# Row sums of a 64 MB tensor: 16-row loads from two queues, and a finely cut last buffer

## Chip, cores, metric

One core of a Trainium2 chip is used. The metric is the device time of one execution, in microseconds (us), as the median of several runs.

## The reference

```python
def setup_inputs():
    batch, seq, dim = 32, 512, 1024
    return {"x": np.random.randn(batch, seq, dim).astype(np.float32)}

def reference(x):
    return np.sum(x, axis=-1).astype(np.float32)
```

There are 16,384 rows of 1,024 floats, 67.1 MB. Each of the 128 partitions gets 128 consecutive rows. The result is 64 KB.

## The kernel before

Fifteen tiles of 8 rows a partition (4 MB each) are loaded by one queue, that of SyncE, into four buffers. VectorE sums four rows of each tile in one reduction, ScalarE the other four, one activation with an accumulator a row. The sixteenth tile is loaded row by row, and the two engines take the rows in turn.

```python
    G = 8
    ...
    T = C // G              # C = 128 rows a partition, so 16 tiles
    DVE_N = 4
    ...
    xpool = ctx.enter_context(tc.tile_pool(name="x", bufs=4))
    ...                     # res, and the two helpers: one activation a row; one reduction of n rows
    for t in range(T):
        xt = xpool.tile([P, G, D], x.dtype, tag="xt")
        c0 = t * G
        if t < T - 1:
            nc.sync.dma_start(out=xt, in_=x_t[t])
            reduce_cols_dve(xt[:, 0:DVE_N], c0, DVE_N)
            for j in range(DVE_N, G):
                reduce_col_act(xt[:, j], c0 + j)
        else:
            for j in range(G):
                nc.sync.dma_start(out=xt[:, j], in_=x_t[t, :, j])
            ...             # even rows on ScalarE, odd rows on VectorE
    nc.sync.dma_start(out=out2d, in_=res)
```

A scheduler puts the instructions of each engine into an order of its own, within what the data dependences allow.

Of the kernel before, what the change touches and what calls it, by code (L numbers as in the profile page):

```python
# [1 line left out]

# [4 lines left out]


@with_exitstack
def kernel(  # L10
    ctx: ExitStack,
    tc: tile.TileContext,
    x: bass.AP,
    out: bass.AP,
):
    nc = tc.nc
    P = nc.NUM_PARTITIONS

    x_flat = x.flatten_outer_dims()
    R, D = x_flat.shape  # L20
    assert R % P == 0
    C = R // P

    G = 8
    assert C % G == 0
    T = C // G
    DVE_N = 4

    x_t = x_flat.rearrange("(p t j) d -> t p j d", p=P, j=G)

    out2d = out.rearrange("a (b c) -> (a b) c", c=C)

    xpool = ctx.enter_context(tc.tile_pool(name="x", bufs=4))
    rpool = ctx.enter_context(tc.tile_pool(name="res", bufs=1))

    res = rpool.tile([P, C], mybir.dt.float32)

    def reduce_col_act(xt_col, c):
        nc.scalar.activation(  # L39
            out=xt_col,  # L40
            in_=xt_col,
            func=mybir.ActivationFunctionType.Copy,
            accum_out=res[:, c : c + 1],
        )

    def reduce_cols_dve(xt_cols, c0, n):
        nc.vector.tensor_reduce(  # L47
            out=res[:, c0 : c0 + n],
            in_=xt_cols,
            axis=mybir.AxisListType.X,  # L50
            op=mybir.AluOpType.add,
        )

    for t in range(T):
        xt = xpool.tile([P, G, D], x.dtype, tag="xt")
        c0 = t * G
        if t < T - 1:
            nc.sync.dma_start(out=xt, in_=x_t[t])  # L58
            reduce_cols_dve(xt[:, 0:DVE_N], c0, DVE_N)
            for j in range(DVE_N, G):  # L60
                reduce_col_act(xt[:, j], c0 + j)
        else:
            for j in range(G):
                nc.sync.dma_start(out=xt[:, j], in_=x_t[t, :, j])
            for j in range(G):
                if j % 2 == 0:
                    reduce_col_act(xt[:, j], c0 + j)
                else:
                    reduce_cols_dve(xt[:, j], c0 + j, 1)

    nc.sync.dma_start(out=out2d, in_=res)


# [1 line left out]
_INS = ['x']  # L75
_OUTS = [((32, 512), 'float32')]


# [23 lines left out]
```

## Time and profile before

| what | value |
|---|---|
| time, median | 165.22 us (165.18 to 165.25) |
| profiled span | 163.7 us |
| VectorE busy, ScalarE busy | 71.0 us, 69.6 us (43% each) |
| interval between landings of 4 MB tiles | 9.73 us, so 431 GB/s |

The first fence is the part of the page that cuts the span into 40 equal slices. A digit is the busy share of a slice in tenths; DMA is the mean share of the 16 DMA engines, and GB/s is what they moved.

```profile
DVE  0006337091551907337090642808245190733952
ACT  3006337091551907336091642808145190733960
DMA  6999999999999999999999999999999999998980
GB/s 200 432 432 440 416 448 416 416 432 424 424 424 440 416 448 424 416 456 424 432 442 416 448 416 424 448 432 432 432 424 448 416 424 448 424 432 364 407 349 16
```

The DMA row reads 8 or 9 from the second slice to the last but one; the two compute rows are full only in single slices, with nearly empty ones between. The second fence is the chain of work that ended last, by line, as shares of the span.

```profile
DMA xt<-in_x_dram 88%; DVE res L47 9%; SPq L58 1%
```

The waits view names the engine and tile that waited, what it waited for, the total in us, the count and the longest.

```profile
DVE res L47 <- DMA xt<-in_x_dram: 90.3, 17, 13.6
ACT xt L39 <- DMA xt<-in_x_dram: 89.6, 16, 11.5
```

Both compute engines spend some 90 us waiting for loads. The timeline gives start, duration, engine, line, operation, and in brackets the idle time before it and what ended it.

```profile
13.56 4.42 DVE L47 TENSOR_REDUCE res<-xt 128x4 f32<-128x4096 f32 x1 [13.56 <-DMA xt<-in_x_dram]
23.24 4.42 DVE L47 TENSOR_REDUCE res<-xt 128x4 f32<-128x4096 f32 x1 [5.26 <-DMA xt<-in_x_dram]
...
149.86 6.67 DVE L47 TENSOR_REDUCE res<-xt 128x4 f32<-128x4096 f32 x3 [5.30 <-DMA xt<-in_x_dram]
...
160.04 1.22 DVE L47 TENSOR_REDUCE res<-xt 128x1 f32<-128x1024 f32 x1 [1.28 <-DMA xt<-in_x_dram]
161.33 0.35 SPq L71 DMA_DIRECT2D out_dram<-res  x1
```

The tiles land 9.7 us apart and take 4.42 us to sum. After the last landing (160.04) there is one reduction of 1.22 us, and then the store. So the kernel is a load of 67 MB at 431 GB/s, with the DMA engines busy all the time (share 0.99 to 1.02 in the windows from 4 to 148 us), with a start of about 2 us and an end of about 4 us.

### The profile page before, as it was taken

The numbers are of one execution on the slowest core, as the hardware profiler recorded it, in microseconds if no ns is written. First come the engines' busy times: TensorE is split into PE (matmuls) and PEld (weight loads), VectorE is DVE, ScalarE is ACT, GpSimd is POOL, SyncE is SP. The second block draws the span as 40 slices with busy tenths as digits, with TensorE's granted clock in tenths as the row PEclk, the third lists the DMA queues.
The fourth block names the chain that finished last, engine by engine and source line by source line (L and its number), as shares of the span: only waits on it lengthen the run. The fifth ranks groups of instructions, "written<-read, shape, count | busy, mean of one in ns | idle before, by whom it ended". The sixth has DMA issues, their size and how long they took to land.

```text
span 163.7 us, 243 instructions
## 1 busy us (share of the span) xinstructions
DVE 71.0 (43%) x19; ACT 69.6 (43%) x129; POOL 0.2 (0%) x4
## 2 busy tenths in 40 slices
DVE  0006337091551907337090642808245190733952
ACT  3006337091551907336091642808145190733960
POOL 0000000000000000000000000000000000000000
DMA  6999999999999999999999999999999999998980
GB/s 200 432 432 440 416 448 416 416 432 424 424 424 440 416 448 424 416 456 424 432 442 416 448 416 424 448 432 432 432 424 448 416 424 448 424 432 364 407 349 16
DMA packets 3457, 67.18 MB, mean 410 GB/s; under 512 B 384, under 2 KB 512, under 8 KB 1536
## 3 DMA queue, kind: packets, MB, share of 16 engines
q1 hardware_dynamic: 3456, 67.18, 96.5%
q14 instruction: 1, 0.01, 0.0%
HBM read 67.11 MB, written 0.07 MB: 410 GB/s over the span
## 4 chain that ended last, share of the span: by engine, by line
DMA 88%; DVE 9%; SPq 1%; issue 0%
DMA xt<-in_x_dram 88%; DVE res L47 9%; SPq L58 1%
## 5 line engine op out<-in xcount | busy, mean ns | idle before, releaser
L47 DVE TENSOR_REDUCE res<-xt 128x4 f32<-128x4096 f32 (+1 forms) x19 | 71.0, 3745 | 90.3 <-DMA xt<-in_x_dram 90.3
L39 ACT ACTIVATE xt<-xt 128x1024 f32<-128x1024 f32 x64 | 66.8, 1044 | 89.6 <-DMA xt<-in_x_dram 89.6
L39 ACT ACTIVATION_READ_ACCUMULATOR xt<-xt 128x1 f32 x64 | 11.9, 187 | 0.0
L39 ACT ACT_TABLE_LOAD x1 | 1.3, 1283 | 0.7 <-PEq L86 0.7
L86 POOL MEMSET const-bfloat16-1.0<- 128x1 bf16 x1 | 0.1, 101 | 0.0
L86 POOL MEMSET const-uint8-127<- 128x1 uint8 x1 | 0.1, 101 | 0.0
L86 POOL MEMSET const-float32-0.0<- 128x1 f32 x1 | 0.1, 98 | 0.2 <-issue 0.2
L86 POOL MEMSET const-float32-1.0<- 128x1 f32 x1 | 0.1, 98 | 0.0
## 6 DMA issues: line engine op xcount, KB each, us to landing
xt<-in_x_dram SPq DMA_DIRECT2D x15, 4096.0 KB, 34.4
xt<-in_x_dram SPq DMA_DIRECT2D x8, 512.0 KB, 27.0
out_dram<-res SPq DMA_DIRECT2D x1, 64.0 KB, 1.5
```

What stands on the lines that cost most here:

```text
L39: nc.scalar.activation(out=xt_col, in_=xt_col, func=mybir.ActivationFunctionType.Copy, accum_out=res[:, c : c + 1],)
L47: nc.vector.tensor_reduce(out=res[:, c0 : c0 + n], in_=xt_cols, axis=mybir.AxisListType.X, op=mybir.AluOpType.add,)
L58: nc.sync.dma_start(out=xt, in_=x_t[t])
L86: nc = _bacc.Bacc("TRN2", target_bir_lowering=False, num_devices=1)
```

## The change

The intent was to use two issuing queues and larger transfers, and to make the work behind the last landing small. Tiles have 16 rows (8 MB) in three buffers, and the loads are issued in turn by SyncE and ScalarE. The last tile comes in pieces of 8, 4, 2, 1, 1/2, 1/4 and 1/4 rows. The last row is summed on VectorE by an operation that reads two streams, adds them and accumulates.

```diff
-    G = 8
+    G = 16
-    xpool = ctx.enter_context(tc.tile_pool(name="x", bufs=4))
+    xpool = ctx.enter_context(tc.tile_pool(name="x", bufs=3))
+    queues = [nc.sync, nc.scalar]
+    issued = []
+    def load(xt, c0, a, b):
+        q = queues[len(issued) % 2 if len(issued) < T else 0]
+        issued.append(a)
+        q.dma_start(out=xt[:, a:b], in_=x_p[:, c0 * D + a : c0 * D + b])
...
+    def pairs_dve(xt, a, b, first, acc):
+        h = (b - a) // 2
+        nc.vector.tensor_tensor_reduce(out=xt[:, a : a + h], in0=xt[:, a : a + h],
+            in1=xt[:, a + h : b], scale=1.0, scalar=first, op0=ADD, op1=ADD, accum_out=acc)
...
+    for t in range(T - 1):
+        ...
+        load(xt, c0, 0, G * D)
+        rows_dve(xt, c0, 0, G // 2)
+        rows_act(xt, c0, G // 2, G // 2)
...
+    for n in (8, 4, 2, 1):
+        load(xt, c0, j * D, (j + n) * D)
+        ...
+    cuts = [j * D + k for k in (0, D // 2, 3 * D // 4, D)]
+    for a, b in zip(cuts, cuts[1:]):
+        load(xt, c0, a, b)
...
+    for i, (a, b) in enumerate(zip(cuts, cuts[1:])):
+        pairs_dve(xt, a, b, acc[i - 1] if i else 0.0, acc[i])
```

Tiles 0, 2, 4 and 6 and the small pieces fall to SyncE. Tiles 1, 3 and 5 and the 8-row piece fall to ScalarE, which also sums rows. The scheduler's order on ScalarE, with L for a load and S for the eight row sums of a tile, is: L1, S0, S1, L3, S2, S3, S4, L5, L(8-row piece), S5, S6, and the sums of the pieces.

More of the change, by code (lines that the diff above doesn't have):

```diff
@@ L6 @@
 from concourse._compat import with_exitstack
+F32 = mybir.dt.float32
+ADD = mybir.AluOpType.add
 @with_exitstack
@@ L22 @@
     C = R // P
-    G = 8
+    x_p = x_flat.rearrange("(p c) d -> p (c d)", p=P)
+    out2d = out.rearrange("a (b c) -> (a b) c", c=C)
+    G = 16
     assert C % G == 0
     T = C // G
-    DVE_N = 4
-    x_t = x_flat.rearrange("(p t j) d -> t p j d", p=P, j=G)
-    out2d = out.rearrange("a (b c) -> (a b) c", c=C)
-    xpool = ctx.enter_context(tc.tile_pool(name="x", bufs=4))
+    xpool = ctx.enter_context(tc.tile_pool(name="x", bufs=3))
     rpool = ctx.enter_context(tc.tile_pool(name="res", bufs=1))
-    res = rpool.tile([P, C], mybir.dt.float32)
@@ L38, in reduce_col_act @@
-    def reduce_col_act(xt_col, c):
-        nc.scalar.activation(
-            out=xt_col,
-            in_=xt_col,
-            func=mybir.ActivationFunctionType.Copy,
-            accum_out=res[:, c : c + 1],
-        )
-    def reduce_cols_dve(xt_cols, c0, n):
-        nc.vector.tensor_reduce(
-            out=res[:, c0 : c0 + n],
-            in_=xt_cols,
-            axis=mybir.AxisListType.X,
-            op=mybir.AluOpType.add,
-        )
-    for t in range(T):
-        xt = xpool.tile([P, G, D], x.dtype, tag="xt")
+    res = rpool.tile([P, C], F32, name="res")
@@ new lines, with rows_dve @@
+    part = rpool.tile([P, 4], F32, name="part")
+    queues = [nc.sync, nc.scalar]
[4 more added lines that the diff above has]
+        q.dma_start(out=xt[:, a:b], in_=x_p[:, c0 * D + a : c0 * D + b])
+    def rows_dve(xt, c0, j, n):
+        nc.vector.tensor_reduce(
+            out=res[:, c0 + j : c0 + j + n],
+            in_=xt[:, j * D : (j + n) * D].rearrange("p (j d) -> p j d", d=D),
+            axis=mybir.AxisListType.X,
+            op=ADD,
+        )
@@ new lines, in rows_act @@
+    def rows_act(xt, c0, j, n):
+        for i in range(j, j + n):
+            v = xt[:, i * D : (i + 1) * D]
+            nc.scalar.activation(
+                out=v,
+                in_=v,
+                func=mybir.ActivationFunctionType.Copy,
+                accum_out=res[:, c0 + i : c0 + i + 1],
+            )
+    def pairs_dve(xt, a, b, first, acc):
+        h = (b - a) // 2
+        nc.vector.tensor_tensor_reduce(
+            out=xt[:, a : a + h],
+            in0=xt[:, a : a + h],
+            in1=xt[:, a + h : b],
+            scale=1.0,
+            scalar=first,
+            op0=ADD,
+            op1=ADD,
+            accum_out=acc,
+        )
@@ L56 @@
+    for t in range(T - 1):
         c0 = t * G
-        if t < T - 1:
-            nc.sync.dma_start(out=xt, in_=x_t[t])
-            reduce_cols_dve(xt[:, 0:DVE_N], c0, DVE_N)
-            for j in range(DVE_N, G):
-                reduce_col_act(xt[:, j], c0 + j)
-        else:
-            for j in range(G):
-                nc.sync.dma_start(out=xt[:, j], in_=x_t[t, :, j])
-            for j in range(G):
-                if j % 2 == 0:
-                    reduce_col_act(xt[:, j], c0 + j)
-                else:
-                    reduce_cols_dve(xt[:, j], c0 + j, 1)
+        xt = xpool.tile([P, G * D], F32, tag="xt", name="xt")
+        load(xt, c0, 0, G * D)
+        rows_dve(xt, c0, 0, G // 2)
+        rows_act(xt, c0, G // 2, G // 2)
@@ new lines @@
+    c0 = (T - 1) * G
+    xt = xpool.tile([P, G * D], F32, tag="xt", name="xt")
+    j = 0
+    runs = []
+    for n in (8, 4, 2, 1):
+        load(xt, c0, j * D, (j + n) * D)
+        runs.append((j, n))
+        j += n
+    cuts = [j * D + k for k in (0, D // 2, 3 * D // 4, D)]
+    for a, b in zip(cuts, cuts[1:]):
+        load(xt, c0, a, b)
+    for j, n in runs:
+        if n > 1:
+            rows_dve(xt, c0, j, n // 2)
+            rows_act(xt, c0, j + n // 2, n // 2)
+        else:
+            rows_act(xt, c0, j, 1)
@@ L71 @@
+    acc = [part[:, 0:1], part[:, 1:2], res[:, C - 1 : C]]
+    for i, (a, b) in enumerate(zip(cuts, cuts[1:])):
+        pairs_dve(xt, a, b, acc[i - 1] if i else 0.0, acc[i])
     nc.sync.dma_start(out=out2d, in_=res)
```

## The prediction

> **What bounds the kernel now.** Loads. In the chain of waits, 88% of the span (163.7 us) is the load of xt. VectorE and ScalarE are 43% busy each; the waits view puts their idle time (90.3 and 89.6 us) on that load. In the timeline a 4 MB load lands every 9.73 us (13.56 to 149.86, 14 intervals): 431 GB/s, with the DMA engines at about 1.00 share in the windows view. Only the ends are open: about 2 us before data flows, and after the last landing (160.02) one 1.22 us reduction and 2.4 us for the store. The eight pieces at the end run at about 408 GB/s.
>
> **What the change removes or adds.** At the ends, little: the last VectorE work shrinks from 1.22 to about 0.5 us (estimate); larger pieces save perhaps 0.3 us. About -1 us.
>
> What it moves is worse. An 8 MB load needs 19.5 us at 431 GB/s. [...] So two loads in flight land together, at half rate each, with one more in reserve (three buffers). Summing a tile takes about 8.7 us on VectorE (4.42 us per 4 rows) and 8.3 us on ScalarE (1.04 us a row).
>
> Moreover a load issued by ScalarE sits in its instruction stream. In the changed kernel's instruction order, tile 3's load stands behind ScalarE's sums of tiles 0 and 1, and the loads of tile 5 and the 8-row piece behind those of tiles 3 and 4, though tile 5's buffer (tile 2's) has long been free.
>
> Estimate of the walk, from these durations:
> - Tiles 0 and 1 land together near 43 us, tile 2 near 62. Tiles 3 and 4 are issued near 60, just in time.
> - Tiles 3 and 4 land together near 101. Tile 6 cannot be issued until tile 3 is summed (110), tile 5 until ScalarE has also summed tile 4 (118). DMA is idle about 11 us from 100.
> - Tile 6 lands (144) before tile 5 (154 to 160), but both engines take tile 5 first. Then tile 5, tile 6 and the pieces are summed back to back: 8.7+8.7+4.4+2.3+1.2+1.3, about 26.6 us after tile 5's landing. Compute, not DMA, ends the kernel; the quarter-row pieces gain nothing.
> - Sums end at 181 to 187, span 183 to 189, time (span + 1.5) 184.6 to 190.5.
>
> **Predicted time: 186 us**, range 176 to 192 (8 in 10). Chances: faster by over 2%: 0.02; within 2%: 0.06; slower: 0.92.
>
> **What would show it.**
> - First sums start near 43 us, not 13.6, tiles 0 and 1 almost together (served by issue time: near 23).
> - GB/s row: near 430 until 100 us, a hole of about 10 us, then near 430 to about 165.
> - Waits: tile 6's issue waits on sums of tile 3; VectorE's longest wait about 40 us.
> - The chain ends in over 20 us of back-to-back VectorE or ScalarE work.
> - VectorE busy still about 70 us; an 8-row reduction 8.7 us.
>
> **What would make it wrong.** If the engines serve the earlier-issued load first, tile 0 lands near 23 us, the hole vanishes, and only the late tile 5 with its serial tail costs: about 171 us. [...] If two queues or 64 KB runs raised the rate above 431 GB/s, each 1% would save 1.5 us. A same or faster result needs both queues to drain in issue order and tile 5 issued early.

Tile 5 at 154 to 160 us, plus 26.6 us of sums, is 181 to 187 us; 2 us to the end of the span and 1.5 us from span to time make 184.6 to 190.5 us, and the point was 186 us. The 0.5 and 0.3 us at the ends are estimates that start from the 1.22 us and the 408 GB/s of the trace before.

## The result, and the profile after

| | before | after |
|---|---|---|
| time, median | 165.24 us (165.18 to 165.28) | 177.11 us (177.09 to 177.31) |
| profiled span | 163.7 us | 175.5 us |
| ratio | | 1.0727, 95% interval 1.0711 to 1.0742 |

A ratio is the mean time of one kernel's fast runs over that of the other's in the same rounds, so it is not quite the ratio of the medians quoted. An interval that holds 1 means that the two are not told apart.

The 40 slices of the changed kernel (one slice is 4.39 us):

```profile
DVE  0000000003999607910001999700000005999994
ACT  2000000003999507910001999600000005999992
DMA  6999999997999997999879509999999899998600
GB/s 239 478 478 403 388 403 478 478 433 329 433 478 478 463 403 329 480 478 478 373 343 478 239 0 478 388 388 418 478 478 403 388 403 422 426 452 375 237 0 15
```

The DMA row now has a hole: in the slice that begins at 101 us nothing moved. After 165 us it is empty while both compute rows still read 9. Some windows around those places, in the form start:end, length, then busy us and instruction count of VectorE, ScalarE and GpSimd, then granted clock, DMA share and GB/s:

```profile
100.00:104.00 4.00, 4.00 (x1) 4.00 (x8) 0.00 (x0) 1.00 0.00 0
104.00:108.00 4.00, 4.00 (x2) 4.00 (x9) 0.00 (x0) 1.00 0.70 262
...
160.00:166.00 6.00, 6.00 (x2) 6.00 (x13) 0.00 (x0) 1.00 0.83 332
166.00:174.00 8.00, 6.98 (x9) 6.04 (x12) 0.00 (x0) 1.00 0.00 1
```

Nothing moved from 100 to 104 us, and practically nothing after 166 us while VectorE worked on for 7 us. The waits are now few and long:

```profile
DVE res L48 <- DMA xt<-in_x_dram: 103.8, 4, 42.5
```

VectorE has four waits, the longest 42.5 us, against 17 of at most 13.6 us. The chain in order of time (start, us, what) shows what the waits have to do with ScalarE:

```profile
0.73 41.77 DMA xt<-in_x_dram
...
42.52 10.54 ACT xt L58 x21
...
53.11 42.67 DMA xt<-in_x_dram
...
95.81 4.87 ACT xt L58 x9
...
100.92 5.43 ACT xt L58 x12
...
106.39 40.58 DMA xt<-in_x_dram
...
146.99 18.53 DVE res L48 x3
```

Three long loads, of which the second and the third were each released by a run of ScalarE's row sums (x21 and so on counts trace records; a row sum leaves two), and then a long run of sums that waits for no load. The timeline, cut to the same places, shows the issues of ScalarE's queue (ACTq) between its sums:

```profile
42.53 17.28 DVE L48 TENSOR_REDUCE res<-xt 128x8 f32<-128x8192 f32 x2 [42.53 <-DMA xt<-in_x_dram]
...
52.94 1.04 ACT L58 ACTIVATE xt<-xt 128x1024 f32<-128x1024 f32 x1
53.11 0.33 ACTq L45 DMA_DIRECT2D xt<-in_x_dram  x1
...
66.74 8.69 DVE L48 TENSOR_REDUCE res<-xt 128x8 f32<-128x8192 f32 x1 [6.93 <-DMA xt<-in_x_dram]
...
95.81 17.28 DVE L48 TENSOR_REDUCE res<-xt 128x8 f32<-128x8192 f32 x2 [20.39 <-DMA xt<-in_x_dram]
...
106.39 0.34 ACTq L45 DMA_DIRECT2D xt<-in_x_dram  x1
...
146.99 24.92 DVE L48 TENSOR_REDUCE res<-xt 128x8 f32<-128x8192 f32 x5 [33.91 <-DMA xt<-in_x_dram]
...
173.12 0.35 SPq L107 DMA_DIRECT2D out_dram<-res  x1
```

SyncE's two issues that matter, of tile 4 and of tile 6 (merged with the pieces):

```profile
59.89 0.33 SPq L45 DMA_DIRECT2D xt<-in_x_dram  x1
```

```profile
104.57 10.99 SPq L45 DMA_DIRECT2D xt<-in_x_dram  x6
```

Tile 5's buffer was free at 75.4 us, when tile 2 had been summed (66.74 + 8.69). Its load was issued at 106.39 us, when ScalarE's sequencer had got past the sums of tiles 3 and 4. It landed at 146.99 us, and 26 us of back-to-back sums followed, to 173.05 us. The costs of single operations, from the groups of instructions (busy us and mean ns between the bars):

```profile
L48 DVE TENSOR_REDUCE res<-xt 128x8 f32<-128x8192 f32 x7 | 60.5, 8681 | 103.8 <-DMA xt<-in_x_dram 103.8
...
L67 DVE CUSTOM_DVE_ANT_0 xt<-xt,part 128x128 f32<-128x128 f32 x2 | 0.7, 352 | 0.1
...
L67 DVE CUSTOM_DVE_ANT_0 xt<-xt 128x256 f32<-128x256 f32 x1 | 0.4, 416 | 0.0
```

The DMA records in the trace show how the engines shared their time (they were read from the trace itself and are not one of the views, so no fence shows them). A record is one contiguous run of one partition, 64 KB long here. Counted in order of their start, the first records of the changed kernel are:

```
queue     records   start of first and last of the group, us
SyncE      16        1.74   2.89
ScalarE    16        4.80   5.81
SyncE      16        7.22   8.22
ScalarE    16        9.63  10.64
SyncE      16       12.05  13.06
```

The records come in groups of 16, as many as there are DMA engines, and the last record of a group starts when the last of the group before ends (both at 5.81 us for the second group). By this order each engine took one 64 KB record from one queue (2.42 us, the median) and the next from the other. So both tiles ran at half rate: tile 0's records took 38.0 us (1.74 to 39.71), where with one queue a tile landed every 19.4 us (first experiment). Tile 0's last data record ended at 39.71 us, but its 16 completion records ran only from 41.35 us on, each behind one more record of the other queue, and its sums began at 42.53 us.

### The profile page after: what moved, and what is told of

It reads as the page before. It is cut to its first block, busy times and chain, and to the rows that moved or that the text cites. A ratio compares the mean times of both kernels' runs of the same rounds, so it can differ in the third digit from the quotient of the medians.

```text
span 175.5 us, 218 instructions
## 1 busy us (share of the span) xinstructions
DVE 69.2 (39%) x16; ACT 68.2 (39%) x129; POOL 0.2 (0%) x4
## 4 chain that ended last, share of the span: by engine, by line
DMA 71%; DVE 13%; ACT 12%; issue 2%; another core or an unknown queue 0%; DVEq 0%
DMA xt<-in_x_dram 71%; DVE res L48 12%; ACT xt L58 12%; DVE xt L67 0%; DVE part L67 0%; DVEq L67 0%; DVEq L133 0%
## 5 line engine op out<-in xcount | busy, mean ns | idle before, releaser
L48 DVE TENSOR_REDUCE res<-xt 128x8 f32<-128x8192 f32 (+3 forms) x10 | 68.2, 6866 | 103.8 <-DMA xt<-in_x_dram 103.8
L58 ACT ACTIVATION_READ_ACCUMULATOR xt<-xt 128x1 f32 x64 | 11.9, 187 | 0.0
L67 DVE CUSTOM_DVE_ANT_0 xt<-xt,part 128x128 f32<-128x128 f32 x2 | 0.7, 352 | 0.1
```

The costliest lines, as they stand in the source:

```text
L48: nc.vector.tensor_reduce(out=res[:, c0 + j : c0 + j + n], in_=xt[:, j * D : (j + n) * D].rearrange("p (j d) -> p j d", d=D), axis=mybir.A ...
L58: nc.scalar.activation(out=v, in_=v, func=mybir.ActivationFunctionType.Copy, accum_out=res[:, c0 + i : c0 + i + 1],)
L67: nc.vector.tensor_tensor_reduce(out=xt[:, a : a + h], in0=xt[:, a : a + h], in1=xt[:, a + h : b], scale=1.0, scalar=first, op0=ADD, op1=A ...
```

## The experiments

The theory after the result has three parts.

- **Place in the stream**: a load issued by ScalarE cannot leave before ScalarE's sequencer has got past the sums ahead of it. It is late although its buffer is free (tile 5: free at 75.4, issued at 106.39 us).
- **Sharing**: two queues make tiles land in pairs, which brings compute and freed buffers late and in lumps (tiles 0 and 1 were summed in one run of 17.28 us from 42.53 us on).
- **The end**: when tile 5 lands late, the sums of tiles 5, 6 and 7 come after the loads and not beside them (26 us of sums from 146.99 us on).

The rivals: 16-row tiles in three buffers are too coarse in any case; sharing alone makes the loss; ScalarE's queue is slower in itself.

### One queue

```diff
-        q = queues[len(issued) % 2 if len(issued) < T else 0]
+        q = nc.sync
```

> All loads from SyncE, all else as in the changed kernel. Theory (two queues: loads shared packet by packet, and the loads of ScalarE stuck behind its sums): loads land one after the other again, first sums near 23 us, no hole in the DMA row, sums of tile 5 start near 120 us and not 147, about 164.5 us (163 to 166). Rival (16-row tiles with three buffers are too coarse, whatever the queue): stays near 177 us.

Measured: 164.17 us (164.01 to 164.19), ratio to before 0.9932 (0.9916 to 0.9949). The timeline:

```profile
23.14 8.69 DVE L48 TENSOR_REDUCE res<-xt 128x8 f32<-128x8192 f32 x1 [23.14 <-DMA xt<-in_x_dram]
42.54 8.69 DVE L48 TENSOR_REDUCE res<-xt 128x8 f32<-128x8192 f32 x1 [10.71 <-DMA xt<-in_x_dram]
...
139.50 8.69 DVE L48 TENSOR_REDUCE res<-xt 128x8 f32<-128x8192 f32 x1 [10.66 <-DMA xt<-in_x_dram]
149.22 4.42 DVE L48 TENSOR_REDUCE res<-xt 128x4 f32<-128x4096 f32 x1 [1.03 <-DMA xt<-in_x_dram]
...
159.55 0.35 DVE L67 CUSTOM_DVE_ANT_0 xt<-xt,part 128x128 f32<-128x128 f32 x1
```

The tiles land 19.4 us apart (432.6 GB/s over the six intervals from 23.14 to 139.50) and there is no hole. The rival of coarse tiles falls: with one queue, the same tiles, buffers and sums are a little faster than before. All of the loss, and more, goes with the second queue, that is with the sharing and the places of ScalarE's loads together.

### Two queues, with ScalarE's loads early

The same split of the loads over the queues as in the change. The loop issues the load of tile t+3 right behind the sums of tile t, and loads, activations and reductions are pinned to program order.

```diff
+    for t in range(3):
+        start(t)                     # allocate the buffer and load
     for t in range(T - 1):
-        load(xt, c0, 0, G * D)
         rows_dve(...)
         rows_act(...)
+        if t + 3 < T:
+            start(t + 3)
```

> Both queues as in the changed kernel, but each load of ScalarE stands in its stream directly behind the sums that free its buffer (tile 3 behind tile 0, tile 5 behind tile 2, the 8-row piece behind tile 4). If the place in the stream makes most of the loss: about 167.5 us (166 to 170), no hole, still the first sums near 42 us; what is left over the one-queue run (about 3 us) is the sharing. If the sharing alone makes the loss: near 177 us. If the place alone makes it: the same as the one-queue run.

Measured: 165.22 us (165.08 to 165.35), ratio to before 0.9999 (0.9984 to 1.0013), which is below the 166 to 170 us expected.

```profile
42.48 17.28 DVE L51 TENSOR_REDUCE res<-xt 128x8 f32<-128x8192 f32 x2 [42.48 <-DMA xt<-in_x_dram]
...
51.25 0.34 ACTq L46 DMA_DIRECT2D xt<-in_x_dram  x1
...
77.85 0.33 ACTq L46 DMA_DIRECT2D xt<-in_x_dram  x1
...
132.19 8.69 DVE L51 TENSOR_REDUCE res<-xt 128x8 f32<-128x8192 f32 x1 [15.51 <-DMA xt<-in_x_dram]
...
152.22 7.74 DVE L51 TENSOR_REDUCE res<-xt 128x4 f32<-128x4096 f32 x3 [0.45 <-DMA xt<-in_x_dram]
```

The pairs still land together (42.48), but tile 5's load leaves at 77.85 us. The loss of 11.9 us is gone. So the places of the loads made it, or the pins, which also fix the order of the sums; the run that puts tile 5 back (below) has the same pins and is slow. Sharing costs what remains over one queue, 165.22 - 164.17 = 1.05 us, a third of the 3 us expected. The DMA records say where it sits: the last load record ended at 158.68 us here and at 158.73 us with one queue, so sharing lost no bandwidth. But the last sum ended at 161.09 against 159.91 us, because ScalarE's 8-row piece shared the engines with the smaller pieces of SyncE and landed at 152.22 instead of 149.22 us; the smaller pieces then waited behind its sums (7.74 us in one run of three reductions).

### All loads from ScalarE, early

```diff
-        q = queues[len(issued) % 2 if len(issued) < T else 0]   # of the run above
+        q = nc.scalar
```

> All loads from ScalarE, each directly behind the sums that free its buffer. No sharing, only the detour through ScalarE's stream. Theory: the same as the one-queue run on SyncE, about 164.5 us, within 1 us. Rival (ScalarE is in itself a worse issuer: its queue is slower, or issuing costs it sums): over 167 us.

Measured: 164.06 us (163.91 to 164.21), ratio to before 0.9928 (0.9914 to 0.9943). This equals the one-queue run on SyncE. Here ScalarE is as good an issuer as SyncE if each load stands where it can leave: its issues (0.33 us of its sequencer each) did not show in the time.

### All loads from ScalarE, where the scheduler puts them

```diff
-        q = queues[len(issued) % 2 if len(issued) < T else 0]   # of the changed kernel
+        q = nc.scalar
```

The resulting order is L0, L1, S0, S1, L2, L3, S2, S3, L4, L5, S4, S5, L6 and so on, though buffers allow L2 at the start.

> All loads from ScalarE where the scheduler puts them: those of tiles 2 and 3 behind the sums of tiles 0 and 1, of tiles 4 and 5 behind those of 2 and 3, and so on. No sharing, but late loads. Theory: three holes of about 4 us each in the DMA row, near 42, 85 and 128 us (each after two tiles landed, until ScalarE has come within about 5 row sums of the end of the second), about 176 us (173 to 179). If only sharing costs: near 164.5 us.

Measured: 179.52 us (179.38 to 179.89), ratio to before 1.0868 (1.0851 to 1.0884). With a single queue and nothing shared this is slower than the change itself. It differs from the run above only by the places of the loads and the pins that fix them, and is 15.5 us slower.

```profile
42.51 8.69 DVE L48 TENSOR_REDUCE res<-xt 128x8 f32<-128x8192 f32 x1 [10.75 <-DMA xt<-in_x_dram]
...
44.60 1.04 ACT L58 ACTIVATE xt<-xt 128x1024 f32<-128x1024 f32 x1
44.73 0.82 ACTq L45 DMA_DIRECT2D xt<-in_x_dram  x2
...
67.17 8.69 DVE L48 TENSOR_REDUCE res<-xt 128x8 f32<-128x8192 f32 x1 [15.97 <-DMA xt<-in_x_dram]
```

In the DMA records nothing was in flight from 42.19 to 45.71, 86.18 to 89.93 and 130.16 to 134.01 us: 3.5, 3.8 and 3.9 us, as expected. But each gap lengthened the interval between landings by more, from 19.4 to 24.6 us (24.66 from 42.51 to 67.17, then 24.57 and 24.62), so by about 5.2 us, and three times that is 15.6 us, the loss within its spread. The rest of each gap is in the ramps: the engines stopped and started over about 1 us each, and the first records after the gap took 2.7 to 2.9 us (medians of 16) instead of 2.42. The expectation of 176 us left that out and was low.

The fence also shows how far ScalarE's sequencer runs ahead of its engine. The load issue at 44.73 us stood behind eight sums, of which two had ended and the third had begun at 44.60: it passed five sums that were still to start. In the changed kernel it is the same: at 53.11 us the eleventh of 16 sums was running (52.94). So it is at 106.39 us, and in the next run at 103.98 us, where the pins fix the load behind all 16 sums.

### Only tile 5's load late again

The early version of both queues with one thing put back: the loads of tile 5 and of the 8-row piece stand behind the sums of tiles 3 and 4.

```diff
-        if t + 3 < T:
-            start(t + 3)
+        for s in {0: [3], 1: [4], 4: [5, 6, 7]}.get(t, []):
+            start(s)
```

> The early version of both queues (165.2 us) with one thing put back: the load of tile 5, and with it the 8-row piece, stands behind ScalarE's sums of tiles 3 and 4 again; tile 3's load stays early. Theory (the late load of tile 5 is what costs): tile 5 is issued near 102 us and not 78, lands near 143, 26 us of sums follow, about 174 us (171 to 177). Rival (it was the late tile 3, or the free order of the other instructions): stays near 165 us.

Measured: 174.54 us (174.37 to 174.78), ratio to before 1.0538 (1.0510 to 1.0566).

```profile
93.40 17.28 DVE L51 TENSOR_REDUCE res<-xt 128x8 f32<-128x8192 f32 x2 [15.71 <-DMA xt<-in_x_dram]
...
103.98 0.34 ACTq L46 DMA_DIRECT2D xt<-in_x_dram  x1
...
144.47 24.93 DVE L51 TENSOR_REDUCE res<-xt 128x8 f32<-128x8192 f32 x5 [33.79 <-DMA xt<-in_x_dram]
```

Tile 5 was issued at 103.98 and landed at 144.47 us, both within 2 us of what was written down. By the ratios (1.0538 against 0.9999, of 165.3 us) this one place makes 8.9 us of the 11.9 us. The rest goes with what still differs from the change: tile 3's load at 53.11 instead of 51.17 us, and the pins. In the traces tile 3 landed 2.4 us earlier here (93.40 against 95.81), tile 5 was issued 2.4 us earlier and landed 2.5 us earlier, so most of that rest is tile 3's load. This run and the early one were in different sets and on different chips, so only the ratios are compared.

### The kernel before with two queues

```diff
-            nc.sync.dma_start(out=xt, in_=x_t[t])
+            (nc.sync if t % 2 == 0 else nc.scalar).dma_start(out=xt, in_=x_t[t])
```

> The kernel before with its fifteen 4 MB loads issued in turn from SyncE and ScalarE, the order left to the scheduler, which puts the ScalarE loads in pairs behind two to four tiles of sums. Theory: the same fault in a finer form; with four buffers of half the size the late loads cost less than in the changed kernel, no large hole but sums queued up at the end, about 168.5 us (166 to 172). If two queues harm only 16-row tiles: 165.2 us, no difference.

Measured: 167.78 us (167.53 to 168.51), ratio to before 1.0136 (1.0104 to 1.0168). The DMA row has no hole; the loss sits at the end, where VectorE's sums run without a pause to the store:

```profile
150.57 13.25 DVE L47 TENSOR_REDUCE res<-xt 128x4 f32<-128x4096 f32 x6 [6.47 <-DMA xt<-in_x_dram]
```

So the fault does not need 16-row tiles, and with 8-row tiles, four buffers and the old end it is smaller. The run does not separate the sharing from the late loads. In this set of runs before itself varied more than elsewhere (165.16 to 166.36 us), hence the wider intervals.

### The end, and the larger transfers

Three kernels take the change's other parts singly, all on SyncE's queue. Kernel "new tail" is before with only its last tile in pieces of 4, 2, 1, 1/2, 1/4 and 1/4 rows and the two-stream sums. Kernel "last row whole" loads and sums the last row of that as one piece. Kernel "half loads" is the one-queue run with each 16-row load issued as two of 8 rows, so that records are 32 KB again.

```diff
# new tail, against the changed kernel
-    G = 16
+    G = 8
...
-    xpool = ctx.enter_context(tc.tile_pool(name="x", bufs=3))
+    xpool = ctx.enter_context(tc.tile_pool(name="x", bufs=4))
...
-        q = queues[len(issued) % 2 if len(issued) < T else 0]
+        q = nc.sync
...
-    for n in (8, 4, 2, 1):
+    for n in (4, 2, 1):
# last row whole, against new tail
-    for a, b in zip(cuts, cuts[1:]):
-        load(xt, c0, a, b)
+    load(xt, c0, j * D, (j + 1) * D)
...
-    for i, (a, b) in enumerate(zip(cuts, cuts[1:])):
-        pairs_dve(xt, a, b, acc[i - 1] if i else 0.0, acc[i])
+    rows_dve(xt, c0, G - 1, 1)
# half loads, against one queue
-        q.dma_start(out=xt[:, a:b], in_=x_p[:, c0 * D + a : c0 * D + b])
+        cut = [a, (a + b) // 2, b] if b - a == G * D else [a, b]
+        for lo, hi in zip(cut, cut[1:]):
+            q.dma_start(out=xt[:, lo:hi], in_=x_p[:, c0 * D + lo : c0 * D + hi])
```

> The 8-row tiles, four buffers and the one queue of before; only the last tile is loaded in pieces of 4, 2, 1, 1/2, 1/4 and 1/4 rows and summed as in the changed kernel. If the 1.1 us that the one-queue run gained over before comes from the end: about 164.3 us, as there. If it comes from the 16-row loads: near 165.2 us.

> As the run with the old loop and the new end, but the last row is loaded whole and summed by one reduction of 1.22 us instead of three pieces with two-stream sums. If the split of the last row is worth what its last sum is shorter (1.22 against about 0.4 us): 0.3 to 0.8 us slower than that run, 164.6 to 165.1 us; if the three dependent sums and the extra loads eat it up: the same.

Measured: new tail 165.36 us (164.71 to 165.67), ratio 0.9977 (0.9951 to 1.0003); last row whole 165.59 us (165.16 to 165.69), ratio 0.9992 (0.9968 to 1.0017). This was the set that varied more, and both medians lie above what was expected. Both intervals hold 1, and they overlap each other, so what the split of the last row is worth stays open. The first was repeated in another set of rounds, beside the one-queue kernel and the one with half loads:

> The one-queue kernel (164.2 us) with every 16-row load issued as two loads of 8 rows, so that a packet is 32 KB again; buffers, sums and the end stay. If the larger packets made the part of the gain that the new end does not (32 KB took 1.213 us and 64 KB 2.418 us in the traces, over the whole input 0.5 us): about 0.5 us slower than the repeated one-queue run of this call, 164.5 to 164.9 us. If packets do not matter: the same.

> The one-queue kernel again, unchanged, beside the other two on this chip: 164.2 us, 0.6 to 0.8% under before.

> The kernel before with the new end only, unchanged from the earlier run that was unclear (ratio 0.998): 0.3 to 0.6 us faster than before, and the rest of the one-queue run's 1.1 us belongs to the larger packets.

| kernel, five rounds together | time, us | ratio to before |
|---|---|---|
| before | 165.13 (164.98 to 165.48) | |
| new tail | 164.52 (164.43 to 164.63) | 0.9965 (0.9952 to 0.9977) |
| half loads | 164.66 (164.56 to 164.69) | 0.9971 (0.9958 to 0.9983) |
| one queue | 164.06 (163.93 to 164.24) | 0.9937 (0.9923 to 0.9950) |

The one-queue gain of 1.1 us repeats. The new end makes about 0.6 us of it. The rest, 0.6 us against half loads and 0.5 us against new tail, goes with the larger loads: with 32 KB records the two kernels are alike, whatever the tile size. In the DMA records a 32 KB record took 1.213 us and a 64 KB record 2.418 us; for the 128 records of 32 KB that each engine would move in all that is 128 x (1.213 - 1.209) = 0.5 us. These are medians of records. The last load record itself ended only 0.3 us later (159.08 with half loads and 159.05 with new tail, against 158.74 us). Halving the records also doubles the number of loads, and no run separates the two.

The one-queue kernel thus beats both given kernels, 0.6 to 0.7% under before; the version with all loads from ScalarE, placed early, equals it.

## Why the prediction was right, and where its size was off

The direction and the causes held: slower, by the late loads of ScalarE, a hole in the loads, and sums without loads at the end. The 177.11 us lie in the range of 176 to 192, near its lower edge, but below the 184.6 to 190.5 us of the walk itself; the point of 186 us was 9 us too slow.

| step of the prediction | predicted | measured |
|---|---|---|
| first sums | near 43 us | 42.53 |
| tile 2 lands | near 62 us | 66.74 |
| tile 3 and tile 4 issued | both near 60 us | 53.11 and 59.89 |
| tile 3 lands | near 101 us | 95.81 |
| tile 6 issued, tile 5 issued | 110 and 118 us | 104.57 and 106.39 |
| DMA idle | about 11 us | 5.3 us (100.20 to 105.53 in the DMA records) |
| tile 6 lands | 144 us | 143.6 (last completion record) |
| tile 5 lands | 154 to 160 us | 146.99 |
| sums from there to the end | 26.6 us | 26.05 us |
| end of sums | 181 to 187 us | 173.05 us |
| VectorE's longest wait, an 8-row reduction | about 40 us, 8.7 us | 42.5 us, 8.68 us |

The mis-sized term is the moment of ScalarE's issues: "tile 5 until ScalarE has also summed tile 4 (118)". The prediction let a load leave when the sums ahead of it were *done*. The runs show it leaving while five row sums ahead of it are still to start (at 53.11 us the eleventh of 16 was running); why it leaves then they do not show. Sixteen sums from 42.52 us would end near 59.2 us (16 x 1.04); the issue came at 53.11 us, 6.1 us before. So tile 3 landed 5 us early, which brought tile 6's issue forward by 5 us and halved the hole. It also made tile 2 late (66.74 instead of 62 us), because tile 3's load, issued at 53.11 us, shared the engines with it (its first record started at 58.28 us, when tile 2 had one group of 16 records still to start). That tile 6's landing agrees is luck: issued 5 us early, it shared with tile 5 almost from its start (first records at 105.53 and 111.07 us). For tile 5 the lead applies a second time: 118 - 106.39 = 11.6 us, of which 5.2 us are tile 3's early landing and 6.1 us the lead itself. The transit of tile 5's load was right (40.6 us against 36 to 42), and so was the tail.

What the loss consists of, by comparing the change with its early version (165.22 us): the last load record ended at 165.63 instead of 158.68 us, 6.9 us later, of which 5.3 us is the hole and the rest its ramps (by the records, five tiles' worth of bytes were in at 100.2 against 100.3 us, six at 126.7 against 119.6, so nothing was lost before the hole); and the sums ran on for 7.4 us behind it instead of 2.4 us. Together this is 6.9 + 5.0 = 11.9 us, the difference of the two times (177.11 - 165.22).

The small gains were about right. "About -1 us" for the end and the larger pieces, where they are not buried, came out as 1.1 us in the one-queue run: 0.6 us from the end and 0.5 to 0.6 us with the larger loads, for which the prediction had "perhaps 0.3 us". The estimate of about 0.5 us for the last VectorE work was somewhat above the 0.36 us measured (352 ns, and an accumulator read of 84 ns that begins before that ends). That sharing alone costs little was not in the prediction at all; it cost 1.05 us. The prediction's 171 us for loads served in order of issue, with the same late tile 5, was tested by no run.

## What to carry to other kernels

In these runs a transfer issued by ScalarE between its sums left when ScalarE's stream reached it and not when its buffer was free (tile 5: free at 75.4, issued at 106.39 us): read the scheduled order of the engine, and put each load directly behind the work that frees its buffer, or give it to an engine without work. One queue that never ran dry already filled the DMA engines here (431 to 433 GB/s); a second one gained no bandwidth (last load record at 158.68 against 158.73 us) and made tiles land in pairs. Fine pieces at the end gained nothing where larger ones were still waiting to be summed: in the changed kernel the last had landed by 165.63 us, and the sums ran on to 173.05.
